# RWKV mixer: low-rank products in two passes over high and low parts, and unit norms of k made in the projections

## The chip, the cores and the metric

The kernel runs on one core of a Trainium2 chip. A time is the device time of one execution in microseconds (us). The kernel before has a median of 3618.76 us over 3 runs (3618.49 to 3623.94).

## The reference, cut to what matters

The model has two blocks. The first holds a mixer of attention and mLSTM, an MLP, an RWKV mixer and a second MLP; the second block has gated linear attention and a mixture of experts. Only the RWKV mixer is touched here. It works on 768 tokens (512 latent, 256 context) of width 1024, that is 16 heads of 64.

```python
def rwkv_prepare(h, mu, w_rkv, w0, w1, w2, a0, a1, a2, g1, g2, k_k, k_a):
    xx = centred_shift(h) - h
    xr, xw, xk, xv, xa, xg = h[None] + xx[None] * mu[:, None, None, :]
    r, k, v = jnp.einsum('sbtd,sde->sbte', jnp.stack([xr, xk, xv]), w_rkv)
    w_logit = w0[:, None, None, :] + jnp.einsum('zbtr,zrd->zbtd', jnp.tanh(jnp.einsum('btd,zdr->zbtr', xw, w1)), w2)
    decay = jnp.exp(-jnp.exp(-jax.nn.softplus(-w_logit.astype(jnp.float32)) - 0.5))
    a = jax.nn.sigmoid(a0[:, None, None, :] + jnp.einsum('zbtr,zrd->zbtd', jnp.einsum('btd,zdr->zbtr', xa, a1), a2))
    g = jax.nn.sigmoid(xg @ g1) @ g2
    kk = split_heads((k * k_k).astype(jnp.float32), RW_HEADS, RW_HEAD_DIM)
    kk = (kk / jnp.maximum(jnp.linalg.norm(kk, axis=-1, keepdims=True), 1e-12)).reshape(k.shape)
    k_dir = k[None] * (1.0 + (a - 1.0) * k_a)
    return r, k_dir, v, decay, -kk, kk[None] * a, g
```

The index z is the direction of the recurrence (forward, backward), the rank r is 64. Each head then runs a recurrence over the tokens in both directions with a 64 x 64 state: `s = s * w + (s a) b' + v k'`, and reads it with r.

## The kernel before, in words

Tensors lie transposed: 128 channels (one feature block f, two heads) on the partitions and 768 tokens along the free axis. `PARTS` cuts the tokens into 512 and 256, one PSUM bank each.

*Projections* (`rw_mixer`). `stream(i, parts)` makes the shifted input of one projection (L1159, VectorE) and splits it into a high part xh (ScalarE, rounded to fp32r) and the rest xl (VectorE). `split` and `load_w` do the same with weights, the low part on GpSimd (L479). `dense` multiplies high by high, high by low and low by high in fp32r passes (L500). `project` yields the PSUM tile of each block; the order of the streams is k, v, w1, a1, r, g1. `keep` copies a block out and stores it. For k, `sqk` is the square of k times `k_k`, and a product with the constant `kks` (L1189) sums the squares of each head into two held banks. After the last block a square root (L1193), a maximum (L1194) and a reciprocal (L1195) leave the inverse norms of all 16 heads in `kkn`. `tw` and `ta` are the 2 x 64 inner values of the two low-rank pairs, in fp32, direction z on partitions 64z to 64z + 63.

*Recurrences* (`rw_scan`). A block is loaded by `head(f)`: k, v, r, and 128 x 128 blocks `w2` and `a2`. The product with the constant `kkb` (L1318) spreads the block's two inverse norms over its 128 channels, and VectorE multiplies (L1319) to get `nkk`. `rw_pre(j)` handles one direction z of one block (j = 2f + z). In it `lora2` makes one fp32 product of contraction 64 for each part (L1446), and ScalarE evicts it with a tanh (L1447). Then come a running sum along the tokens (`cs`), exponentials (L1456, L1457), the scaled operands (L1484 to L1497), Gram products (L1532), an inverse by halves (L1600 to L1635), the outputs (L1681 to L1769), and the chain of states S (L1354, L1362). `rw_pre` of j + 3 is written beside the work on j, so that the pieces of several j overlap; each engine takes its instructions in one fixed order, settled when the program is built.

*PSUM in the recurrences*: banks of tag b rotate by two among L1318, L1446, the Gram products and the chain. The 19 memsets of L1271 clear the block-diagonal tiles on GpSimd before the first block. `keep = {KD-2: tw, KD-1: ta}` in `rw_scan` reuses `tw` and `ta` for the outputs of the last two blocks.

Of the kernel before, what the change touches and what calls it, by code (L numbers as in the profile page):

```python
# [10 lines left out]
F32 = mybir.dt.float32  # L11
F32R = mybir.dt.float32r
# [7 lines left out]
T = 512  # L20
# [97 lines left out]
def constants_rw():  # L118
# [12 lines left out]
    ks = np.zeros((128, 2, 32)); kb = np.zeros((128, 2, 128))  # L131
    for i in range(2):
        for h in range(2):
            ks[64 * h:64 * h + 64, i, 2 * i + h] = 1.0
            kb[2 * i + h::32, i, 64 * h:64 * h + 64] = 1.0
    b.add("kks", ks)
    b.add("kkb", kb)
# [108 lines left out]
def layout(v):  # L246
# [21 lines left out]
    for n in ("w2", "a2"):  # L268
        o["rw_" + n] = np.ascontiguousarray(v["rw_" + n][0].reshape(128, D))
# [43 lines left out]
class Kern:  # L313
# [336 lines left out]
    def ab_mixer(self):  # L650
# [24 lines left out]
        with ExitStack() as st:  # L675
            cp = st.enter_context(tc.tile_pool(name="ab_c", bufs=1, reuse_waits="tile"))
            pool = st.enter_context(tc.tile_pool(name="ab", bufs=2, reuse_waits="tile"))
# [343 lines left out]
    def ml_head(self, h, qkv, ntile, tmp, out):  # L1021
# [34 lines left out]
        for n in range(6):  # L1056
            for d in range(2):
# [11 lines left out]
                if n < 5:  # L1069
                    ns = self.small.tile([128, 130], F32, tag="cst", name=self.uid("cst"), bufs=4)  # L1070
# [6 lines left out]
                if n:  # L1077
                    t = self.small.tile([128, 130], F32, tag="hin", name=self.uid("hin"), bufs=2)
                    nc.scalar.activation(t, pn[:, 130:260], AF.Copy, scale=col("wi", c, d))
                    nc.vector.tensor_tensor(num[d][:, c, :], pn[:, :130], t, op=ALU.add)  # L1080
# [31 lines left out]
    def rw_mixer(self):  # L1112
# [3 lines left out]
        with ExitStack() as st:  # L1116
# [8 lines left out]
            spill = {n: [dr.tile([128, TT], F32, name=f"d_{n}{f}") for f in range(8)] for n in ("x", "r", "k", "v", "g", "o")}  # L1125
            tw = cp.tile([128, TT], F32, name="tw")
            ta = cp.tile([128, TT], F32, name="ta")
            kkn = cp.tile([128, TT], F32, name="kkn")
            with tc.tile_pool(name="rw1", bufs=2, reuse_waits="tile") as pool:
# [45 lines left out]
                def keep(n, f, ps, lo, hi):  # L1175
                    t = pool.tile([128, TT], F32, tag="tmp", name=self.uid("keep"), bufs=self.tb)
                    nc.scalar.activation(t[:, lo:hi], ps[:, lo:hi], AF.Copy)
                    nc.sync.dma_start(spill[n][f][:, lo:hi], t[:, lo:hi])

                act = stream(2, PARTS)  # L1180
                self.x = None
                ssk = [self.bank("ssk"), self.bank("ssk")]
                for f, ps in project(act, self.i["rw_k"], KD, PARTS):
                    keep("k", f, ps, 0, TT)
                    sq = pool.tile([128, TT], F32, tag="tmp", name=self.uid("sqk"), bufs=self.tb)
                    nc.scalar.activation(sq, ps, AF.Square, scale=self.p("k_k")[:, f:f + 1])
                    g = f % 4
                    for q, (a, b) in enumerate(PARTS):
# [3 lines left out]
                for q, (a, b) in enumerate(PARTS):  # L1192
# [1213 lines left out]
```

## Time and profile before

| | |
|---|---|
| median of 3 runs | 3618.76 us |
| profiled execution | 3612.26 us |
| its span | 3610.2 us |
| TensorE clock, mean over the span | 0.956 of full |
| projections of RWKV | 1172 to 1476 us |
| recurrences of RWKV | 1476 to 2249 us |
| output projection, MLP, second block | from 2249 us |
| DMA traffic in the 36th to 39th of 40 slices | 421 GB/s |

The profiled execution is 2.06 us longer than its span. Busy time counts instructions that work on data; an engine's idle time is what it waits. A busy TensorE does not mean a TensorE at full speed: the granted clock is read beside it.

### The profile page before, as it was taken

To read this page: it belongs to the slowest core of one execution; us is meant where nothing else is said; L and a number is where in the kernel's file an instruction comes from. 1 tells how busy PE (TensorE), PEld (TensorE's weight loads), DVE (VectorE), ACT (ScalarE), POOL (GpSimd) and SP (SyncE) were. 2 spreads that over 40 slices of the span, in tenths; PEclk is the share of its full clock that TensorE was granted. 3 is DMA by queue.
4 is the path that set the end of the run, shared out by engine and by line. 5 is a ranking of instruction groups with operands and counts; after the bars stand their busy time and mean duration, and the time that the engine had idled before them with its cause. 6 is when DMAs were issued, how large, how long until landed. Compare 5 with 4: busy or idle time off the path is not lost. (4 is left out here: it accounts for less than half of the span.)

```text
span 3610.2 us, 56697 instructions
## 1 busy us (share of the span) xinstructions
PE 3285.7 (91%) x23614; PEld 2459.9 (68%) x23614; DVE 1748.3 (48%) x3056; ACT 1303.4 (36%) x2465; POOL 898.1 (25%) x460
## 2 busy tenths in 40 slices
PE   7999999999999898799999998889999989799887
PEld 5767887888888676477777776677878767433333
DVE  5475564861322324576666674474333564222213
ACT  3332453221222324376667765322233453100001
POOL 1111113232223422422222220444452334200000
PEclk9999999999999899699999998999999999899999
DMA  5212222552213122100000002475331226699998
GB/s 215 99 65 82 82 71 94 198 170 65 65 60 116 62 90 75 56 15 21 21 21 21 21 8 68 135 231 177 95 127 64 69 87 230 254 421 421 421 421 317
DMA packets 125071, 480.86 MB, mean 133 GB/s; under 512 B 13232, under 2 KB 24944, under 8 KB 100496
## 3 DMA queue, kind: packets, MB, share of 16 engines
q1 hardware_dynamic: 118688, 469.68, 35.9%
q8 instruction: 186, 3.05, 0.3%
q0 software_dynamic: 1184, 4.20, 0.3%
q10 hardware_dynamic: 4944, 3.36, 0.3%
q14 instruction: 69, 0.57, 0.0%
HBM read 451.50 MB, written 25.69 MB: 132 GB/s over the span
## 5 line engine op out<-in xcount | busy, mean ns | idle before, releaser
L479 POOL TENSOR_TENSOR wl<-w,wh 128x1024 fp32r<-128x1024 f32 (+1 forms) x258 | 617.4, 2395 | 1633.9 <-ACT wh L478 1477.8
L478 ACT ACTIVATE wh<-w 128x1024 fp32r<-128x1024 f32 (+1 forms) x258 | 265.8, 1032 | 950.1 <-PE dn L500 332.0
L500 PE MATMUL dn<-hh,wh 128*128 128x512 f32 (+1 forms) x768 | 234.1, 359 | 14.2 <-ACT hh L478 14.2
L500 PE MATMUL up<-ah,wh 128*128 128x512 f32 (+1 forms) x768 | 235.1, 361 | 7.2 <-DVE x L591 3.0
L500 PE MATMUL up<-ah,wl 128*128 128x512 f32 (+1 forms) x768 | 236.0, 362 | 4.8 <-POOL wl L479 4.5
L500 PE MATMUL dn<-hl,wh 128*128 128x512 f32 (+1 forms) x768 | 235.7, 361 | 2.2 <-DVE hl L479 2.2
L500 PE MATMUL dn<-hh,wl 128*128 128x512 f32 (+1 forms) x768 | 234.9, 360 | 2.4 <-POOL wl L479 2.4
L500 PE MATMUL up<-al,wh 128*128 128x512 f32 (+1 forms) x768 | 236.2, 362 | 0.6 <-DVE al L584 0.6
L467 DVE SCALAR_TENSOR_TENSOR side<-wside,condb 128x1024 f32<-128x1024 f32 x128 | 193.2, 1509 | 65.6 <-DMA wside<-ada 64.3
L623 DVE TENSOR_TENSOR u<-u 128x768 f32<-128x768 f32 (+1 forms) x64 | 126.6, 1980 | 131.9 <-ACT u L622 131.9
L591 DVE SCALAR_TENSOR_TENSOR x<-dn,ada,x 128x512 f32<-128x512 f32 x96 | 60.5, 657 | 257.4 <-PE dn L500 257.4
L500 PEld LDWEIGHTS dn<-hh,wh 128*128 128x128 f32 x768 | 128.0, 190 | 39.3 <-ACT hh L478 15.8
L500 PEld LDWEIGHTS up<-ah,wh 128*128 128x128 f32 x768 | 129.0, 191 | 32.8 <-ACT ah L583 3.9
L500 PEld LDWEIGHTS up<-ah,wl 128*128 128x128 f32 x768 | 128.5, 190 | 30.9 <-POOL wl L479 8.5
L500 PEld LDWEIGHTS dn<-hl,wh 128*128 128x128 f32 x768 | 128.7, 190 | 25.6 <-DVE hl L479 4.1
L500 PEld LDWEIGHTS dn<-hh,wl 128*128 128x128 f32 x768 | 128.4, 190 | 26.0 <-POOL wl L479 3.3
L500 PEld LDWEIGHTS up<-al,wh 128*128 128x128 f32 x768 | 129.5, 191 | 23.7 <-DVE al L584 1.8
L500 PE MATMUL rp<-xh,wh 128*128 128x512 f32 (+1 forms) x368 | 112.0, 371 | 23.0 <-ACT xh L478 20.6
L500 PE MATMUL rp<-xl,wh 128*128 128x512 f32 x368 | 113.2, 373 | 13.9 <-DVE xl L479 13.8
L478 ACT ACTIVATE hh<-u 128x768 fp32r<-128x768 f32 (+1 forms) x64 | 47.3, 739 | 217.2 <-DVE u L623 217.2
L500 PE MATMUL p<-ah,wh 128*128 128x512 f32 (+1 forms) x320 | 116.9, 394 | 2.2 <-ACT ah L583 1.2
L500 PE MATMUL rp<-xh,wl 128*128 128x512 f32 x368 | 112.4, 370 | 3.0 <-POOL wl L479 3.0
(612 smaller groups left out, 7471.6 us busy)
## 6 DMA issues: line engine op xcount, KB each, us to landing
w<-mlp SPq DMA_DIRECT2D x128, 512.0 KB, 3.6
wside<-ada SPq DMA_DIRECT2D x96, 512.0 KB, 3.8
ew<-e_gate SPq DMA_DIRECT2D x45, 1024.0 KB, 19.8
ew<-e_up SPq DMA_DIRECT2D x41, 1024.0 KB, 20.6
ew<-e_down SPq DMA_DIRECT2D x39, 1024.0 KB, 19.8
wada<-ada SPq DMA_DIRECT2D x48, 512.0 KB, 3.8
ewm<-e_up SPq DMA_DIRECT2D x18, 1024.0 KB, 19.8
ewm<-e_down SPq DMA_DIRECT2D x18, 1024.0 KB, 19.8
```

Source lines behind the costliest of these rows:

```text
L467: nc.vector.scalar_tensor_tensor(o, w, 1.0, cb[:, q, :], op0=ALU.mult, op1=ALU.mult, accum_out=out[:, f, q:q + 1])
L478: nc.scalar.activation(hi, src, AF.Copy)
L479: (eng or nc.vector).tensor_tensor(lo, src, hi.bitcast(F32), op=ALU.subtract)
L500: nc.tensor.matmul(ps[:, a:b], ww[:, 128 * k:128 * k + 128], aa[:, a:b], start=(first and k == 0 and q == 0), stop=(last and k == nk - 1 a ...
L591: self.nc.vector.scalar_tensor_tensor(x[:, a:b], ps[:, a:b], gt[:, f, q:q + 1], x[:, a:b], op0=ALU.mult, op1=ALU.add)
L623: nc.vector.tensor_tensor(u[:, lo:hi], u[:, lo:hi], u[:, lo:hi], op=ALU.mult)
```

## The change

The second factors of both low-rank pairs come as one array `rw_l2`: for each block 128 x 512, four blocks of 128 columns (two tables, two directions), with the 64 rows repeated on the other 64 partitions. `head` loads it into the tile of tag y and splits it: high part l2h on ScalarE, low part l2l on GpSimd. The inner values become two tiles each, one for a direction: `factors` writes the high part on partitions 64z and following, and the rest on the other 64. A product over all 128 partitions with l2h and one with l2l then sum all four combinations of the parts. The inverse norm is made per block in the projections by `unit`, called one block late, and -k k_k / norm goes to memory and is loaded as `nkk`. Two new tiles `ends` take the place of `tw` and `ta` for the last outputs. The tiles cst and hin of the first mixer move from one pool to another.

```diff
-    for n in ("w2", "a2"):
-        o["rw_" + n] = np.ascontiguousarray(v["rw_" + n][0].reshape(128, D))
+    l2 = np.stack([v["rw_w2"][0], v["rw_a2"][0]])
+    l2 = np.concatenate([l2, l2], 2).reshape(2, 2, 128, KD, 128).transpose(3, 2, 0, 1, 4)
+    o["rw_l2"] = np.ascontiguousarray(l2.reshape(KD, 128, 512))
...
+                def factors(out, ps, func):
+                    t = pool.tile([128, TT], F32, tag="tmp", name=self.uid("fac"), bufs=self.tb)
+                    nc.scalar.activation(t, ps, func)
+                    for z, h in enumerate(out):
+                        r, o = slice(64 * z, 64 * z + 64), slice(64 - 64 * z, 128 - 64 * z)
+                        nc.scalar.activation(h[r], t[r], AF.Copy)
+                        nc.vector.tensor_tensor(h[o], t[r], h[r].bitcast(F32), op=ALU.subtract)
...
-                ssk = [self.bank("ssk"), self.bank("ssk")]
+                def unit(f, t, sq):
+                    for a, b in PARTS:
+                        pk = self.bank("ssk")
+                        nc.tensor.matmul(pk[:, :b - a], C["hones"], sq[:, a:b], start=True, stop=True)
+                        nc.scalar.activation(sq[:, a:b], pk[:, :b - a], AF.Sqrt)
+                    nc.vector.tensor_scalar(sq, sq, 1e-12, -1.0, op0=ALU.max, op1=ALU.mult)
+                    nc.vector.reciprocal(sq, sq)
+                    nc.vector.scalar_tensor_tensor(sq, t, self.p("k_k")[:, f:f + 1], sq, op0=ALU.mult, op1=ALU.mult)
+                    nc.sync.dma_start(spill["kk"][f], sq)
+                late = None
                 for f, ps in project(act, self.i["rw_k"], KD, PARTS):
-                    keep("k", f, ps, 0, TT)
+                    t = keep("k", f, ps, 0, TT)
                     sq = pool.tile([128, TT], F32, tag="tmp", name=self.uid("sqk"), bufs=self.tb)
                     nc.scalar.activation(sq, ps, AF.Square, scale=self.p("k_k")[:, f:f + 1])
...
-                        nc.tensor.matmul(ssk[q][32 * g:32 * g + 32, :b - a],
-                                         C["kks"].rearrange("p (i m) -> p i m", i=2)[:, f // 4, :], sq[:, a:b],
-                                         start=(f < 4), stop=(f >= 4), skip_group_check=True)
+                    if late:
+                        late()
+                    late = partial(unit, f, t, sq)
...
-                    nc.scalar.activation(kkn[:, a:b], ssk[q][:, :b - a], AF.Sqrt)
-                nc.vector.tensor_scalar(kkn, kkn, 1e-12, -1.0, op0=ALU.max, op1=ALU.mult)
-                nc.vector.reciprocal(kkn, kkn)
...
                 for f, ps in project(act, self.i["rw_v"], KD, PARTS):
                     keep("v", f, ps, 0, TT)
+                    if late:
+                        late = late()
...
-                    nc.scalar.activation(tw, ps, AF.Tanh)
+                    factors(tw, ps, AF.Tanh)
...
-                    nc.scalar.activation(ta, ps, AF.Copy)
+                    factors(ta, ps, AF.Copy)
...
         def head(f):
-            w2 = pool.tile([128, 128], F32, tag="w2", name=self.uid("w2"), bufs=1)
-            a2 = pool.tile([128, 128], F32, tag="a2", name=self.uid("a2"), bufs=1)
-            nc.sync.dma_start(w2, self.i["rw_w2"][:, fc])
-            nc.sync.dma_start(a2, self.i["rw_a2"][:, fc])
             nkk = role("nkk")
-            for a, b in PARTS:
-                pk = self.pbank("b")
-                nc.tensor.matmul(pk[:, :b - a], kb[gi:gi + 32, f // 4, :], kkn[gi:gi + 32, a:b], start=True, stop=True)
-                nc.vector.scalar_tensor_tensor(nkk[:, a:b], k[:, a:b], self.p("k_k")[:, f:f + 1], pk[:, :b - a],
-                                               op0=ALU.mult, op1=ALU.mult)
+            nc.sync.dma_start(nkk, spill["kk"][f])
+            raw = role("y", T)
+            nc.sync.dma_start(raw, self.i["rw_l2"][f])
+            wh = pool.tile([128, 4, 128], F32R, tag="l2h", name=self.uid("l2h"), bufs=1)
+            wl = pool.tile([128, 4, 128], F32R, tag="l2l", name=self.uid("l2l"), bufs=1)
+            self.split(raw, wh.rearrange("p n m -> p (n m)"), wl.rearrange("p n m -> p (n m)"), nc.gpsimd)
...
         def lora2(n, t, bias, name):
             o = e1(name)
             for a, b in PARTS:
                 ps = self.pbank("b")
-                nc.tensor.matmul(ps[:, :b - a], w[zr, :], t[zr, a:b], start=True, stop=True)
+                for q, w in enumerate(hd["l2"]):
+                    nc.tensor.matmul(ps[:, :b - a], w[:, 2 * n + z, :], t[z][:, a:b], start=(q == 0), stop=(q == 1))
                 nc.scalar.activation(o[:, a:b], ps[:, :b - a], AF.Tanh, scale=0.5, bias=bias)
```

The order on TensorE at the low-rank products of direction 0 of block 2 (the period from 1615 us), before. The first names are PSUM banks; consts and crw hold constants, ar, kd, bh and ad belong to the outputs of an earlier j:

```order
L1318 MATMUL b_12927<-kkn,crw 128x512
L1715 MATMUL d_13061<-vx_11218,ak_11212 64x64 x4
L1681 MATMUL d_13074<-ar_11741,kd_11208 128x128
L1318 MATMUL b_12930<-kkn,crw 128x256
L1681 MATMUL d_13074<-ar_11741,kd_11208 128x128
L1446 MATMUL b_12934<-tw,w_2026_12922 128x512
L1446 MATMUL b_12937<-tw,w_2026_12922 128x256
L1681 MATMUL d_13074<-ar_11741,kd_11208 128x128 x2
L1446 MATMUL b_12941<-ta,a_2027_12923 128x512
L1446 MATMUL b_12944<-ta,a_2027_12923 128x256
L1746 MATMUL d_13084<-bh_13039,ad_11214 128x128 x4
```

And now (L1452 is the low-rank product, L1687 was L1681, L1752 was L1746, L1710 was L1704):

```order
L1687 MATMUL d_13164<-ar_11825,kd_11287 128x128 x2
L1452 MATMUL b_13020<-tw_9327,l2h_13015 128x512
L1452 MATMUL b_13020<-tw_9327,l2l_13016 128x512
L1687 MATMUL d_13164<-ar_11825,kd_11287 128x128 x2
L1452 MATMUL b_13024<-tw_9327,l2h_13015 128x256
L1452 MATMUL b_13024<-tw_9327,l2l_13016 128x256
L1752 MATMUL d_13174<-bh_13129,ad_11293 128x128
L1452 MATMUL b_13029<-ta_9329,l2h_13015 128x512
L1452 MATMUL b_13029<-ta_9329,l2l_13016 128x512
L1452 MATMUL b_13033<-ta_9329,l2h_13015 128x256
L1452 MATMUL b_13033<-ta_9329,l2l_13016 128x256
L1752 MATMUL d_13174<-bh_13129,ad_11293 128x128 x3
```

The two products with kkn are gone, each low-rank part is a pair of passes, and one more group of other products stands between the parts.

The order on GpSimd at the start of the recurrences, the last of the memsets and what follows, before:

```order
L1271 MEMSET zb_11236 128x1536
L1271 MEMSET zb_11238 128x1536
L1271 MEMSET lo 128x1536
L1494 TENSOR_SCALAR al_11286<-al_11286,half 128x768
L1495 TENSOR_TENSOR al_11286<-al_11286,k_11263 128x768
L1497 TENSOR_TENSOR kd_11206<-al_11286,wl_11279 64x12x64
```

And now:

```order
L1284 MEMSET zb_11315 128x1536
L1284 MEMSET zb_11317 128x1536
L1284 MEMSET lo 128x1536
L474 TENSOR_TENSOR l2l_11352<-y_11349,l2h_11351 128x512
L1500 TENSOR_SCALAR al_11364<-al_11364,half 128x768
L1501 TENSOR_TENSOR al_11364<-al_11364,k_11342 128x768
L1503 TENSOR_TENSOR kd_11285<-al_11364,wl_11355 64x12x64
```

The low part of block 0's weights (l2l) stands behind the memsets and ahead of the first al.

The order on VectorE at the turn from the stream of k to that of v (xs and xl are v's inputs and their low parts), before:

```order
L1159 SCALAR_TENSOR_TENSOR xs_9999<-xx_9363,params,x_4577 128x768
L1194 TENSOR_SCALAR kkn<-kkn 128x768
L479 TENSOR_TENSOR xl_9989<-xs_9987,xh_9988 128x768
L1195 RECIPROCAL kkn<-kkn 128x768
L479 TENSOR_TENSOR xl_9995<-xs_9993,xh_9994 128x768
L479 TENSOR_TENSOR xl_10001<-xs_9999,xh_10000 128x768
```

And now, where sqk_9964 is the unit of block 6:

```order
L1155 SCALAR_TENSOR_TENSOR xs_10052<-xx_9363,params,x_4576 128x768
L1194 TENSOR_SCALAR sqk_9964<-sqk_9964 128x768
L474 TENSOR_TENSOR xl_10048<-xs_10046,xh_10047 128x768
L1195 RECIPROCAL sqk_9964<-sqk_9964 128x768
L474 TENSOR_TENSOR xl_10054<-xs_10052,xh_10053 128x768
L1196 SCALAR_TENSOR_TENSOR sqk_9964<-keep_9961,params,sqk_9964 128x768
L1155 SCALAR_TENSOR_TENSOR xs_10058<-xx_9374,params,x_4577 128x768
```

The reciprocal stands at the same place between v's first two low parts, with another block's data; a multiplication follows the second low part. The reciprocal of block 7 has moved behind the last of v's low parts.

## Rows read from the trace of the kernel before

**Rows 1.** The page, part 1: busy time, share of the span and instructions.

```profile
PE 3285.7 (91%) x23614; PEld 2459.9 (68%) x23614; DVE 1748.3 (48%) x3056; ACT 1303.4 (36%) x2465; POOL 898.1 (25%) x460
```

**Rows 2.** Busy time in stretches of the projections and recurrences: (x) are instructions, then clock.

```profile
1183.00:1476.00 293.00, 257.70 (x1163) 195.10 (x1163) 104.25 (x122) 97.63 (x128) 88.50 (x64) 0.94 0.22 76
1476.50:1541.00 64.50, 40.62 (x369) 28.70 (x367) 39.49 (x53) 25.03 (x58) 32.81 (x23) 0.63 0.15 47
1541.00:1615.10 74.10, 66.29 (x1039) 53.80 (x1038) 53.88 (x87) 53.16 (x141) 23.50 (x11) 0.95 0.05 13
1615.10:1704.30 89.20, 84.44 (x1296) 67.75 (x1296) 62.29 (x122) 63.49 (x160) 20.96 (x10) 0.98 0.07 21
1704.30:1796.30 92.00, 87.68 (x1295) 69.62 (x1295) 62.23 (x121) 63.41 (x160) 20.95 (x10) 0.94 0.07 21
1799.90:1811.00 11.10, 11.10 (x63) 7.51 (x62) 4.83 (x9) 4.65 (x8) 0.00 (x0) 0.54 0.00 0
```

**Rows 3.** Timeline of TensorE, blocks from 1615 and 1796: start, duration, line, form.

```profile
1615.15 1.12 PE L1318 MATMUL b<-kkn,crw 32*128 32x512 f32 x2 [0.24 <-DVE vx L1333]
...
1617.00 0.69 PE L1318 MATMUL b<-kkn,crw 32*128 32x256 f32 x2
...
1618.04 1.55 PE L1446 MATMUL b<-tw,w 64*128 64x512 f32 x4
1619.53 0.71 PE L1681 MATMUL d<-ar,kd 128*128 128x128 f32 x4
...
1802.61 2.93 PE L1446 MATMUL b<-ta,a 64*128 64x512 f32 x4
```

**Rows 4.** Timeline of TensorE in the dense stream of v.

```profile
1299.69 0.52 PE L500 MATMUL rp<-xh,wh 128*128 128x512 f32 x2
1300.05 0.52 PE L500 MATMUL rp<-xl,wh 128*128 128x512 f32 x2
```

**Rows 5.** Timeline of ScalarE at the evictions of the same products.

```profile
1619.26 1.05 ACT L1447 ACTIVATE wl<-b,half 128x512 f32<-128x512 f32 x2 [1.80 <-PE b L1446]
```

**Rows 6.** Timeline of GpSimd at the start of the recurrences.

```profile
1489.87 1.38 POOL L1271 MEMSET lo<- 128x1536 f16 x1
```

**Rows 7.** Groups of GpSimd, shapes apart: count, busy, mean ns, idle before.

```profile
L479 POOL TENSOR_TENSOR wl<-w,wh 128x512 fp32r<-128x512 f32 x16 | 21.2, 1329 | 30.8 <-ACT wh L478 30.4 <-DMA w<-gla_proj 0.5
```

**Rows 8.** Timelines of TensorE and ScalarE at the start of the recurrences.

```profile
1483.05 2.90 PE L1446 MATMUL b<-tw,w 64*128 64x512 f32 x4 [4.76 <-DVE ar L1485]
...
1498.14 2.26 PE L1532 MATMUL b<-ar,bd 128*128 128x128 f32 x9 [4.71 <-DVE bd L1492]
...
1490.62 0.84 ACT L1456 ACTIVATE wl<-cs 128x768 f32<-128x768 f32 x1
```

**Rows 9.** Timelines of VectorE and TensorE at the turn from k to v.

```profile
1281.71 0.96 DVE L479 TENSOR_TENSOR xl<-xs,xh 128x768 fp32r<-128x768 f32 x1 [0.17 <-ACT xh L478]
1282.58 4.95 DVE L1195 RECIPROCAL kkn<-kkn 128x768 f32<-128x768 f32 x1
...
1288.39 1.01 PE L500 MATMUL rp<-xl,wh 128*128 128x512 f32 x2 [3.29 <-DVE xl L479]
```

**Rows 10.** Timelines of VectorE and TensorE at the turn from w1 to a1.

```profile
1373.26 6.81 DVE L1159 SCALAR_TENSOR_TENSOR xs<-xx,params,x 128x768 f32<-128x768 f32 x5
...
1377.70 0.62 PE L500 MATMUL rp<-xh,wh 128*128 128x512 f32 x2 [2.88 <-ACT xh L478]
1380.99 1.01 PE L500 MATMUL rp<-xl,wh 128*128 128x512 f32 x2 [2.68 <-DVE xl L479]
```

**Rows 11.** Timeline of the loads and stores that SyncE issues.

```profile
1749.13 0.32 SPq L1390 DMA_DIRECT2D d_o<-y  x1
...
1758.19 0.33 SPq L1310 DMA_DIRECT2D w<-rw_w  x1
```

**Rows 12.** Line 1492 by itself: count, duration min/median/max, first and last start.

```profile
L1492 DVE SCALAR_TENSOR_TENSOR bd<-nkk,cs x32: 949/1242/2489, 1496.1 to 2141.7; 64x768 f32<-64x768 f32 x32
```

**Rows 13.** The page, part 5: a group of weight loads in a dense stream.

```profile
L500 PEld LDWEIGHTS dn<-hh,wh 128*128 128x128 f32 x768 | 128.0, 190 | 39.3 <-ACT hh L478 15.8
```

More of the change, by code (lines that the diff above doesn't have):

```diff
@@ L130, in constants_rw @@
     b.add("hones", hb)
[L131 to L137, printed above, removed]
     return b
@@ L676, in ab_mixer @@
             cp = st.enter_context(tc.tile_pool(name="ab_c", bufs=1, reuse_waits="tile"))
-            pool = st.enter_context(tc.tile_pool(name="ab", bufs=2, reuse_waits="tile"))
+            pool = self.abp = st.enter_context(tc.tile_pool(name="ab", bufs=2, reuse_waits="tile"))
             nab = self.i["c_ab"].shape[1]
@@ L1069, in ml_head @@
                 if n < 5:
-                    ns = self.small.tile([128, 130], F32, tag="cst", name=self.uid("cst"), bufs=4)
+                    ns = self.abp.tile([128, 130], F32, tag="cst", name=self.uid("cst"), bufs=4)
                     if n == 0:
@@ L1077, in ml_head @@
                 if n:
-                    t = self.small.tile([128, 130], F32, tag="hin", name=self.uid("hin"), bufs=2)
+                    t = self.abp.tile([128, 130], F32, tag="hin", name=self.uid("hin"), bufs=2)
                     nc.scalar.activation(t, pn[:, 130:260], AF.Copy, scale=col("wi", c, d))
@@ L1124, in rw_mixer @@
             H = {n: crh[:, a:b] for n, (a, b) in self.crwh.items()}
[L1125 to L1128, printed above, removed]
+            spill = {n: [dr.tile([128, TT], F32, name=f"d_{n}{f}") for f in range(8)] for n in ("x", "r", "k", "kk", "v", "g", "o")}
+            tw = [cp.tile([128, TT], F32R, name=f"tw{z}") for z in range(2)]
+            ta = [cp.tile([128, TT], F32R, name=f"ta{z}") for z in range(2)]
+            ends = [cp.tile([128, T], F32, name=f"end{i}") for i in range(2)]
             with tc.tile_pool(name="rw1", bufs=2, reuse_waits="tile") as pool:
@@ L1224, in rw_mixer @@
                 self.ps = s2.enter_context(tc.tile_pool(name="ps2", bufs=1, space=PSUM, reuse_waits="tile"))
-                self.rw_scan(pool, C, H, spill, (tw, ta, kkn))
+                self.rw_scan(pool, C, H, spill, (tw, ta, ends))
             self.open_w()
@@ L1237, in rw_mixer @@
                     else:
-                        t = (tw, ta)[k - KD + 2][:, :T]
+                        t = ends[k - KD + 2]
                     h = pool.tile([128, T], F32R, tag="oh", name=self.uid("oh"), bufs=KD)
@@ L1263, in rw_scan @@
         nc = self.nc
-        tw, ta, kkn = small
-        keep = {KD - 2: tw, KD - 1: ta}
+        tw, ta, ends = small
+        keep = {KD - 2: ends[0], KD - 1: ends[1]}
         def diag(n, c=12, dt=F32):
@@ L1445, in lora2 @@
                 ps = self.pbank("b")
[L1446 removed]
+                for q, w in enumerate(hd["l2"]):
+                    nc.tensor.matmul(ps[:, :b - a], w[:, 2 * n + z, :], t[z][:, a:b], start=(q == 0), stop=(q == 1))
                 nc.scalar.activation(o[:, a:b], ps[:, :b - a], AF.Tanh, scale=0.5, bias=bias)
             return o
[L1450 to L1451 removed]
+        sg = lora2(0, per["tw"], half[:, z, f:f + 1], "wl")
+        th = lora2(1, per["ta"], half[:, 2 + z, f:f + 1], "al")
         nc.vector.tensor_scalar(sg, sg, 1.0, None, op0=ALU.add)
```

14 lines of the change are left out of this document (3 added, 11 removed).

## The prediction

> **What bounds the kernel now.** I read the page's busy shares first: TensorE is busy 91% of the span, VectorE 48%, ScalarE 36%, GpSimd 25% [rows 1]. An average is no proof, so I read the stage that the change touches by the busy time of each engine in stretches: the projections of the RWKV mixer, and then the recurrences, one stretch for each feature block f (a pair of heads; its period runs from one broadcast of the k norms to the next) [rows 2]. In blocks 2 to 7 TensorE works 84.4 of 89.2 us or 87.7 of 92.0 us, VectorE 62 and ScalarE 63. The pipeline is not full in block 0 (40.6 of 64.5 us) and nearly full in block 1 (66.3 of 74.1). The end of the program waits for expert weights; their loads follow the stages before them, so I let an earlier end of RWKV come through whole.
>
> The reader is to see a second thing in rows 2: periods of 92.0 us have mean clock 0.94, those of 89.2 us 0.98. The difference is a spell at half clock. The stretch 1799.9 to 1811 has a granted clock of 0.54 and TensorE busy for all of 11.1 us [rows 2]; the low-rank product that takes 1.55 us elsewhere takes 2.93 there [rows 3]. So the engine is at 1.2 GHz instead of 2.4 for about 10 us. The spell begins in the broadcast and the low-rank products of direction 0, in four of blocks 2 to 7 (those from 1704, 1796, 1888 and 2069; the two from 1615 and 1980 have none). It also gives an exchange rate: such a block has 87.68 − 84.44 = 3.24 us more TensorE time and a period 2.8 us longer (92.0 − 89.2), so a microsecond of TensorE is worth some 0.87 of period.
>
> **The change, part by part.** *Broadcast of the k norms (L1318).* For each block two products go, of 512 and 256 columns: 1.12 and 0.69 us [rows 3]. Modelled ends reach past the next start by some 0.06 (the low-rank product from 1618.04 lasts 1.55 and the next begins at 1619.53), so 1.69 us go. The two VectorE multiplications behind them go too; VectorE is not the bound.
>
> *Low-rank products (L1446).* There are four per block, two tables for two directions. One of 512 + 256 columns takes 1619.53 − 1618.04 = 1.49 us to the next start [rows 3]. The nearest fp32r row is the dense stream, where one pass over 512 + 256 columns takes 1300.05 − 1299.69 = 0.36 us [rows 4]; two passes take 0.72 in a stream. A product that stands alone also pays for a change of operands: I add 0.2 us as an estimate (two bare parts, 1.12 + 0.69, cost 0.26 more than the joined 1.55), so 0.92, or 0.57 saved. Four save 2.28 us; one more break in the row order of direction 0 (the order shown with the change) takes 0.2 back. Together with the broadcast: 3.77 us of TensorE per block. Bounds: nothing saved on the low-rank part (1.69 in all) and the pure stream figures (4 × 0.77 + 1.69 = 4.77).
>
> *Eviction.* ScalarE's two tanh of a product take 1.05 us [rows 5], longer than the new 0.92 of TensorE, and two banks rotate. A third part can then wait some 0.3 us for its bank. I count this in the factor 0.87 and not apart.
>
> So blocks 2 to 7 give 6 × 3.77 × 0.87 = 19.7 us. In block 1 the pipeline fills and I take a third, 1.3; block 0 nothing, since TensorE waits there 24 of 64 us. Sum −21.0.
>
> *The spells.* They cost 4 × 2.8 = 11.2 us. The stretch in which they begin loses over a third of its TensorE time, and what is left there runs over all 128 rows of the array rather than 32 or 64. A start that occurs in four blocks of six is near an edge. I take them as gone, −11.2; the other ends are 0 and a loss (third rival).
>
> *Start of the recurrences.* GpSimd's first work there is 19 memsets (L1271); the last ends at 1489.87 + 1.38 = 1491.25 [rows 6]. The low part of block 0's weights is now made on GpSimd, behind all of them in its queue. A split of that size took 1.33 us [rows 7], so it is ready at about 1492.6. Before, the first low-rank product began at 1483.05 and the exponential behind it at 1490.62 [rows 8]. After it: the high passes can go early; the four low passes (0.3), the tanh evictions (two of 1.05 us, about 2.4 with their semaphores) and the table load (1.3, the gap ahead of 1490.62) lead to an exponential at 1496 to 1496.5. So +5.5 us, which the Gram product at 1498.14 [rows 8] follows. Ends: 0, if the memsets start earlier, and 1492.6 − 1483.05 = 9.5.
>
> *Norms made in the projections.* The new unit of a block has an fp32 product of the same columns as the sums that it replaces, two square roots, a scalar operation and a multiplication (about 1.6 with the 0.96 of a 128 × 768 operation), a reciprocal of 4.95 us [rows 9] and a store. Eight units are 52 us of VectorE, in a stage where it works 104 of 293 us [rows 2], and its wait for the k stream covers those of blocks 0 to 5. The unit is delayed by one block, so its product no longer waits for the square. At the turn from k to v the old chain holds TensorE until 1288.39, because the low half of v's second input sits behind the reciprocal from 1282.58 [rows 9]. The new order keeps one reciprocal, block 6's, at that place (order shown), and block 7's comes when v's inputs are made. I take 0, ends −5 and +4. If that cover went, each reciprocal on the path would cost 4.95.
>
> *Splitting tanh(x w1) and x a1.* Each gets two ScalarE copies and two VectorE subtractions over 64 partitions. The nearest row is a VectorE run of five preparing operations, 6.81 us, at 1373.26, after which TensorE waits 2.88 us (for ScalarE) and 2.68 us (for VectorE) [rows 10]: here VectorE does bound. Two subtractions are about 1.9 us by that 0.96. The second turn (a1 to r) is alike. I take +1.5 each, +3; ends 0 and 7.
>
> *Loads of a block.* Two small weight loads become one of 256 KB into the tile of the readout, whose last reader is the store at 1749.13; the old loads went out from 1758.19 on [rows 11] and their use is at 1799. The k norms come as one load more. Landing, and the splits on ScalarE and on GpSimd (1.33 us), have some 40 us; nothing. GpSimd's split can hold VectorE up: L1492 takes 0.95 us at best and 2.49 at worst [rows 12], and GpSimd works 21 us in each block. With 27 us of VectorE free per block I leave that out; were all of it on the path, the sum would lose 8 × 1.33 = 10.6 us.
> The Trainium skill, SBUF — State Buffer, section "Who interferes with whom", says that a VectorE instruction with two inputs in SBUF and a GpSimd one that reads SBUF exclude each other; the spread of L1492 agrees, and at its worst the rule gives those 10.6 us.
>
> **Sum:** −21.0 − 11.2 + 5.5 + 3.0 = −23.7 us on the profiled execution's 3612.26 (its span of 3610.2 and 2.06 around it), giving 3588.6. The median of the runs is 3618.76, 6.5 higher (0.18%); the gain belongs to either, so the forecast is 3595.1. Less than 0.2% (7.2 us) is what a measurement can't tell from no change.
>
> **Rivals.** *First: the spells stay or move.* For it: what is left of the low-rank work is still dense, and nothing else in the block changes. Then −12.5, 3606.3.
>
> *Second: the period is held by the chain of waits, not by TensorE.* VectorE and ScalarE work 62 and 63 of 89 us, much of it one after the other through TensorE; if only a third of the 21.0 us comes through, and the spells' time turns into waiting, the sum is −7 + 8.5 = +1.5, 3620. Against it: the rate of 0.87.
>
> *Third, the slower side: more spells.* The clock falls after every set of low-rank products, 16 of them (two directions, eight blocks), instead of 4, since waits for banks and evictions now stand in them. At 2.8 us each, 12 more cost 33.6 us and the sum is −12.5 + 33.6 = +21, 3640. It decides from eleven spells on (7 more are +19.6 against −12.5, so +7.1). For it: the engine is near the edge. Against: the products of direction 1 have none today.
>
> *Fourth: weight loads exposed.* The dense stream changes weights at each pass, all of 128 rows, and still makes a pass in 0.36 us [rows 4], though a load takes 190 ns [rows 13]. Were each of a product's four loads exposed, it would take 0.92 + 0.76 = 1.68, more than 1.49; a block would save 0.9 instead of 3.77, and with spells as they are the sum is −4.8 + 8.5 = +4, 3622.
> The Trainium skill, TensorE: Matmul & The Clock Gate, section "The mechanism", says that a weight load overlaps running products only where the row group differs, which speaks against this change: its passes use all rows, the old ones half. By that rule 3622; the row has full-height loads hidden, and it decides.
>
> **How the numbers follow.** Forecast 0.46 (own range 3585 to 3603), spells stay 0.26 (3600 to 3613), chain-bound 0.15 (3611 to 3628), more spells 0.09, loads exposed 0.04. The range 3580 to 3615 leaves out the last two and part of the third. Faster: 0.46 + 0.25 + 0.05 of the third = 0.76; same: 0.01 + 0.09 + 0.04 = 0.14; slower: 0.09 + 0.01 = 0.10.
>
> **What would show it.** Right: no L1318; periods of 85 to 86.5 us in blocks 2 to 7, all alike; a low-rank product of 0.9 us; a first exponential near 1496 us, give or take what the projections shift; the last expert loads earlier by the whole gain. Wrong: periods that keep two values some 2.8 us apart (first rival), a period near 89 with TensorE's idle time grown (second), half-clock stretches in every block and direction (third), or 1.7 us per product (fourth).

## The result, and the profile after

The changed kernel has a median of 3583.97 us over 4 runs (3578.87 to 3585.53); the kernel before had 3620.43 (3618.49 to 3623.94) over 4. The ratio is 0.9898, with an interval of 0.9886 to 0.991: some 36 us faster. The two profiled executions stand 28.4 us apart (3612.26 and 3583.87). The profiled execution of before is faster than all of its four timed runs; that of after lies at the median of its own.

First the page's line of busy times, which answers [rows 1]:

```profile
PE 3238.9 (90%) x23582; PEld 2448.4 (68%) x23582; DVE 1791.7 (50%) x3066; ACT 1312.9 (37%) x2491; POOL 908.3 (25%) x468
```

TensorE lost 46.8 us of work, VectorE gained 43. Now the stretches that answer [rows 2], in the same columns; a block's period begins here with its load of v, which before started within half a microsecond of the broadcast from block 2 on:

```profile
1483.40:1543.60 60.20, 27.24 (x246) 20.76 (x246) 30.41 (x43) 20.06 (x44) 33.14 (x23) 0.56 0.21 64
1543.60:1627.30 83.70, 73.41 (x1168) 61.91 (x1166) 61.40 (x93) 60.33 (x161) 25.62 (x13) 0.93 0.06 19
1627.30:1715.40 88.10, 80.75 (x1277) 67.20 (x1277) 65.17 (x120) 62.60 (x158) 21.91 (x11) 0.96 0.09 27
1800.75:1885.74 84.99, 79.22 (x1291) 66.92 (x1291) 60.80 (x120) 63.30 (x161) 22.60 (x11) 0.98 0.10 29
1885.74:1970.74 85.00, 79.21 (x1291) 66.80 (x1291) 60.82 (x120) 63.29 (x161) 22.61 (x11) 0.98 0.10 28
1869.50:1872.90 3.40, 3.40 (x25) 2.67 (x26) 1.90 (x5) 2.11 (x7) 0.00 (x0) 0.50 0.31 87
```

The steady block takes 85.0 us with 79.2 of TensorE, in place of 89.2 with 84.4 or 92.0 with 87.7. The spell of 10 us is gone in all of blocks 2 to 7, but the last row shows that short ones are left: 3.4 us at a granted clock of 0.50, 1.2 GHz, one in each block and two in blocks 2 and 3. Block 1, where before had only two short ones, now holds a long one:

```profile
1562.30:1572.50 10.20, 9.12 (x103) 8.08 (x103) 7.70 (x9) 5.91 (x18) 6.09 (x3) 0.50 0.01 2
```

All periods, from the starts of the loads of v:

| block | 0 | 1 | 2 | 3 | 4 | 5 | 6 |
|---|---|---|---|---|---|---|---|
| before | 53.6 | 83.1 | 89.2 | 92.0 | 92.0 | 92.0 | 89.2 |
| after | 59.7 | 83.7 | 88.1 | 85.4 | 85.0 | 85.0 | 85.0 |

The low-rank products of direction 0 on TensorE, which answer [rows 3]:

```profile
1885.95 0.50 PE L1452 MATMUL b<-tw,l2h 128*128 128x512 f32 x1 [0.24 <-DVE vx L1340]
1886.29 0.40 PE L1452 MATMUL b<-tw,l2l 128*128 128x512 f32 x1
1886.62 0.45 PE L1721 MATMUL d<-vx,ak 128*64 128x64 f32 x8
1887.00 0.71 PE L1687 MATMUL d<-ar,kd 128*128 128x128 f32 x4
1887.69 0.38 PE L1452 MATMUL b<-tw,l2h 128*128 128x256 f32 x1
1887.91 0.28 PE L1452 MATMUL b<-tw,l2l 128*128 128x256 f32 x1
1888.02 0.43 PE L1452 MATMUL b<-ta,l2h 128*128 128x512 f32 x1
```

A pass of 512 columns takes some 0.33 us to the next start here and one of 256 0.11 to 0.22. By themselves, the 16 fp32 low-rank instructions of a block before and the 16 passes now (busy time of TensorE and of its weight loads, then clock):

```profile
1615.10:1704.30 89.20, 6.48 (x16) 2.60 (x16) 0.98 0.07 21
1885.74:1970.74 85.00, 4.22 (x16) 2.59 (x16) 0.98 0.10 28
```

So the passes hold TensorE for 4.2 us; before, the fp32 instructions and the broadcast held it for 6.5 + 1.8 = 8.3.

The start of the recurrences on GpSimd, ScalarE and TensorE, in this order, which answers [rows 6, 8]:

```profile
1493.91 1.37 POOL L1284 MEMSET lo<- 128x1536 f16 x1
1495.25 1.26 POOL L474 TENSOR_TENSOR l2l<-y,l2h 128x512 fp32r<-128x512 f32 x1
...
1491.47 0.63 ACT L473 ACTIVATE l2h<-y 128x512 fp32r<-128x512 f32 x1 [8.48 <-DMA y<-rw_l]
...
1502.20 0.84 ACT L1462 ACTIVATE wl<-cs 128x768 f32<-128x768 f32 x1
...
1492.16 1.00 PE L1452 MATMUL b<-tw,l2h 128*128 128x512 f32 x2 [9.53 <-ACT l2h L473]
1496.56 1.01 PE L1452 MATMUL b<-tw,l2l 128*128 128x512 f32 x2 [3.40 <-POOL l2l L474]
...
1509.72 2.68 PE L1538 MATMUL b<-ar,bd 128*128 128x128 f32 x11 [4.71 <-DVE bd L1498]
```

The high passes went at 1492.16, as soon as ScalarE had split the weights, and the low ones waited 3.40 us for GpSimd, whose split stood behind the memsets. The weights themselves came late: their load is the fifth of the block's six.

### The profile page after: what moved, and what is told of

It reads as the page before. It is cut to its first block, busy times and chain, and to the rows that moved or that the text cites. A ratio compares the mean times of both kernels' runs of the same rounds, so it can differ in the third digit from the quotient of the medians.

```text
span 3581.7 us, 56701 instructions
## 1 busy us (share of the span) xinstructions
PE 3238.9 (90%) x23582; PEld 2448.4 (68%) x23582; DVE 1791.7 (50%) x3066; ACT 1312.9 (37%) x2491; POOL 908.3 (25%) x468
## 5 line engine op out<-in xcount | busy, mean ns | idle before, releaser
L495 PE MATMUL rp<-xh,wh 128*128 128x512 f32 x368 | 111.1, 373 | 23.3 <-ACT xh L473 21.5
L495 PE MATMUL p<-ah,wl 128*128 128x512 f32 x320 | 113.3, 383 | 2.1 <-POOL wl L474 2.1
```

The costliest lines, as they stand in the source:

```text
L495: nc.tensor.matmul(ps[:, a:b], ww[:, 128 * k:128 * k + 128], aa[:, a:b], start=(first and k == 0 and q == 0), stop=(last and k == nk - 1 a ...
```

## The experiments

Profiled executions differ outside the change too: that of after reached the mixer's first instructions 6.3 us late, and gained 6.1 us in the last stage, where the experts' weights came at 426 GB/s instead of 421. So stages are compared below by their own lengths. From the mixer's first instructions to the loads of its output projection after is 28.3 us shorter than before; the other two differences nearly cancel.

**Each half alone.** The low-rank change alone keeps kkn and the broadcast:

```diff
-                nc.tensor.matmul(ps[:, :b - a], w[zr, :], t[zr, a:b], start=True, stop=True)
+                for q, w in enumerate(hd["l2"]):
+                    nc.tensor.matmul(ps[:, :b - a], w[:, 2 * n + z, :], t[z][:, a:b], start=(q == 0), stop=(q == 1))
```

> Only the low-rank products in two passes; the norms of k stay as before (held sums, one reciprocal, two broadcast products per block). Because of memory the output of block 6 goes through DRAM. Theory (the period of a block is TensorE's time, one to one, and the half-clock spell begins in the run of fp32 products over 32 and 64 rows): blocks 2 to 7 without a spell take 85.0 + 1.7 = 86.7 us; with the low-rank products no longer fp32 the run is too short and no 10 us spell is left. Program some 15 us faster than before, 13 slower than the full change. Rival A (the broadcast over 32 rows starts the spells): some blocks at 89 to 90 us, program only 5 to 8 us faster than before. Rival B (a chain of waits sets the period): periods near 85 again, program within 4 us of the full change.

The norms change alone keeps the fp32 products and has `unit` and the load of `nkk`:

```diff
-                nc.tensor.matmul(pk[:, :b - a], kb[gi:gi + 32, f // 4, :], kkn[gi:gi + 32, a:b], start=True, stop=True)
...
+            nc.sync.dma_start(nkk, spill["kk"][f])
```

> Only the norms of k made in the projections; the low-rank products stay fp32 over 64 rows with two small weight loads. Theory: blocks 2 to 7 take 85.0 + 2.4 = 87.4 us without a spell; the first exponential comes some 6 us sooner after the scan's loads than in the full change, and the two splits in the projections are gone (about 3 us); program some 18 us faster than before if the spells go, 8 if they stay. Rival A (the broadcast starts the spells): no spells left, all blocks alike. If the low-rank products alone start them: two kinds of blocks, 87.4 and 90.2. Rival B (chain of waits): periods of 85, program faster than the full change by 9 us.

The low-rank change alone: 3622.57 us, ratio 1.0016 (1.0004 to 1.0027), no gain at all. The norms alone: 3589.76, ratio 0.9916 (0.9902 to 0.9929). A block of each; the first holds one 3.4 us spell (clock 0.98), the second none (1.00):

```profile
1992.78:2081.64 88.86, 81.44 (x1296) 67.62 (x1296) 65.80 (x122) 63.39 (x160) 21.81 (x11) 0.98 0.08 23
```

```profile
1799.88:1886.18 86.30, 81.16 (x1291) 65.83 (x1291) 61.20 (x120) 63.30 (x160) 20.95 (x10) 1.00 0.09 27
```

With the low-rank change alone TensorE worked 81.4 us per block, 3.0 less than before, but the period stayed at 88.9 to 90.9: idle time rose from 4.8 to 7.4 us. So the theory fell for this half. Spells of 6.8 or 10.2 us also stayed in three of its blocks 2 to 6. The norms alone left no spell above 3.4 us in blocks 2 to 6 and added little wait (5.1 us of idle time for 4.8). Their blocks with one short spell (2, 3 and 6) take 87.8 us against 89.2 before, 1.4 us for 1.8 us of broadcast; the blocks at 86.3 have lost the short spell as well. The two gains don't add: the norms alone bring 29 of the 36 us, the low-rank products nothing by themselves and some 6 beside the norms. That long spells stay with the broadcast and go without it is what the rival of the broadcast asked for. Where the low-rank change lost time is in the waits of TensorE, in VectorE's timeline and in GpSimd's (columns of the waits: sum, times, longest):

```profile
PE b L1348 <- DVE vx L1351: 2.1, 1, 2.1
```

```profile
1988.28 2.47 DVE L1559 TENSOR_TENSOR zb<-hi,crwh 64x768 f16<-64x768 f16 x2 [1.24 <-POOL hi L1557]
1990.67 0.95 DVE L1561 TENSOR_TENSOR lo<-Aab,hi 64x768 f16<-64x768 f32 x1
1991.65 0.74 DVE L1351 COPY vx<-b 64x256 f32<-64x256 f32 x2
...
1985.66 2.58 POOL L1557 TENSOR_TENSOR hi<-Aab,crw 64x768 f16<-64x768 f32 x1 [11.79 <-PE b L1566]
1988.32 2.01 POOL L1561 TENSOR_TENSOR lo<-Aab,hi 64x768 f16<-64x768 f32 x1
```

VectorE's two zb operations took 2.47 us together, with GpSimd's lo beside them from 1988.32 on; the copy of v's transposes (vx, 1991.65) came that much later, and TensorE stood 2.1 us. Before, two zb take 1.14 us, and lo waited for TensorE and began only after them:

```profile
1699.59 1.14 DVE L1542 TENSOR_TENSOR zb<-hi,crwh 64x768 f16<-64x768 f16 x2 [1.72 <-POOL hi L1540]
...
1700.97 2.35 POOL L1544 TENSOR_TENSOR lo<-Aab,hi 64x768 f16<-64x768 f32 x1 [1.42 <-PE i L1629]
```

**That meeting taken away.** Both halves of lo on VectorE, on the low-rank change alone:

```diff
-            (nc.gpsimd, nc.vector)[h].tensor_tensor(lo[row(h), :, h, :], Aab[row(h)], hi[row(h), :, h, :], op=ALU.subtract)
+            nc.vector.tensor_tensor(lo[row(h), :, h, :], Aab[row(h)], hi[row(h), :, h, :], op=ALU.subtract)
```

> The low-rank change alone once more, with both halves of `lo` (the low part in the inverse) made on VectorE, so that GpSimd no longer reads memory beside VectorE's zb there. In the low-rank change alone TensorE's busy time fell by 3 us per block against before and its idle time rose by 2.7; zb took 0.89 us on average instead of 0.55, and the transposes of v behind it waited 2.1 us. Theory (the two engines exclude each other there, and that wait ate the gain): zb back at 0.55 us, the wait at L1348 below 0.5 us, undisturbed blocks at 87.3 to 88 us instead of 88.9, program some 8 us faster than the low-rank change alone. Rival (the order of the instructions as a whole makes the waits): zb may shorten, but idle time stays near 7.4 us per block and the period within 0.5 us.

3596.27 us, ratio 0.9939 (0.9922 to 0.9956): 26 us less than the low-rank change alone, three times what was expected. zb, the groups of both kernels over four blocks (count, busy, mean ns), and a block:

```profile
L1559 DVE TENSOR_TENSOR zb<-hi,crwh 64x768 f16<-64x768 f16 x16 | 14.2, 890 | 5.2 <-POOL hi L1557 5.0
```

```profile
L1559 DVE TENSOR_TENSOR zb<-hi,crwh 64x768 f16<-64x768 f16 x16 | 8.9, 553 | 7.2 <-POOL hi L1557 6.8
```

```profile
1718.57:1804.95 86.38, 80.52 (x1296) 67.28 (x1296) 63.82 (x124) 63.42 (x161) 17.83 (x9) 0.98 0.08 23
```

zb is back at 0.55 us, idle time at 5.9 and the period at 86.4. TensorE's busy time fell too, and in blocks 2 to 6 no spell is longer than 3.4 us any more, where the low-rank change alone had three; so the size is not the meeting's alone, and its share is not separated. Two controls make the same edit elsewhere.

> The kernel before, with both halves of `lo` on VectorE: the control of the run in which that move made the low-rank change alone 26 us faster. Theory (the move helped there because GpSimd's lo met VectorE's zb): before has no such meeting (zb 0.55 us), so blocks stay at 89 to 92 us and the program within 5 us of before. Rival (GpSimd's lo costs every version, through its own slowness): blocks 2 to 7 shorter by 1 us and more each, program 6 us or more faster than before.

3619.26 us, ratio 1.0 (0.9988 to 1.0012): where zb and lo don't meet, the edit brings nothing. The traced execution is the slowest of the ten (3637.69), with blocks of 90.2 to 94.9 us, above the 89 to 92 expected.

> The kernel with the early split (block 0's weights first, split on VectorE) with both halves of `lo` on VectorE. Theory (no meeting there): within 3 us of the early split alone. Rival (GpSimd's lo costs every version): 6 us or more faster.

3577.77 us (3574.85 to 3579.74), against 3573.42 (3570.86 to 3577.89) of the same kernel without it (below): 4.4 us slower by the medians, where within 3 were expected, and not the rival's 6 us faster. A small meeting did go there, zb from 0.62 to 0.55 us on average, and brought nothing.

**TensorE's time doubled back.** One low pass more in each low-rank part:

```diff
-                for q, w in enumerate(hd["l2"]):
+                for q, w in enumerate(hd["l2"] + hd["l2"][1:]):
```

> The full change with the low pass done twice (the low part of the weights counts double): four products more passes of 0.36 us, 1.44 us of TensorE per block and nothing else. Theory (rate one to one): periods of 86.4 us in place of 85.0, program 10 to 11 us slower than the full change. By the rate that the prediction took (0.87): 86.25, 9 to 10 us. Rival B (a chain of waits sets the period): 85.0 to 85.3, program within 2 us.

3591.24 us, 7.3 above the change by the medians; the RWKV part of the profiled execution is 9.4 us longer. A block without any spell:

```profile
1889.19:1975.25 86.06, 79.75 (x1299) 66.90 (x1299) 63.46 (x120) 63.93 (x161) 22.28 (x11) 1.00 0.09 28
```

So time added to these products comes through to the end, and the rival that a chain of waits sets the period whatever TensorE does is out. It is no clean one to one: with the early split (below) a block at a clock of 1.00 takes 82.9 us with 77.4 of TensorE, so 2.3 us more of TensorE came with 3.2 us of period, and VectorE's bd grew from 1.60 to 1.98 us on average. A chain that runs through these very products would lengthen too; the run does not part it from TensorE's load.

**The start.** Block 0's weights are loaded first and split on VectorE:

```diff
+            raw = role("y", T)
+            if f == 0:
+                nc.sync.dma_start(raw, self.i["rw_l2"][f])
             r, k, v = role("r", T), role("k"), role("v")
...
-            self.split(raw, wh.rearrange("p n m -> p (n m)"), wl.rearrange("p n m -> p (n m)"), nc.gpsimd)
+            self.split(raw, wh.rearrange("p n m -> p (n m)"), wl.rearrange("p n m -> p (n m)"), nc.gpsimd if f else None)
```

> The full change, but block 0's weights are loaded ahead of its other loads and their low part is made on VectorE, not on GpSimd behind the memsets. Theory (the memsets hold the first low-rank product): its low pass starts at about 1493 instead of 1496.6 or earlier by the load, everything behind it 4 to 5 us sooner, program 4 to 5 us faster than the full change. Rival (something else ends last at the start: the loads of k norms, or GpSimd's queue): the first Gram product moves by less than 1 us and the program by nothing that can be told.

3573.42 us (3570.86 to 3577.89), ratio 0.9872 (0.9857 to 0.9887): the fastest kernel here, 10.5 us under the change and 45.6 under before. VectorE, TensorE and ScalarE at the start:

```profile
1487.88 0.69 DVE L474 TENSOR_TENSOR l2l<-y,l2h 128x512 fp32r<-128x512 f32 x1 [20.61 <-ACT l2h L473]
...
1487.90 1.01 PE L1454 MATMUL b<-tw,l2h 128*128 128x512 f32 x2 [4.36 <-ACT l2h L473]
1488.70 0.93 PE L1454 MATMUL b<-tw,l2l 128*128 128x512 f32 x2
...
1502.29 0.98 PE L1540 MATMUL b<-ar,bd 128*128 128x128 f32 x3 [6.93 <-DVE bd L1500]
...
1495.11 0.84 ACT L1464 ACTIVATE wl<-cs 128x768 f32<-128x768 f32 x1
```

The low passes follow the high ones at once, and block 0 takes 48.6 us in place of 59.7, twice the expected gain: beside the memsets the late load of the weights had cost time. Counted from the load of v, the low passes come 9.3 us sooner and the high ones 5.7; the run changes load and split together and does not part their shares. Blocks 4 to 6 are as in the change, block 2 takes 86.9 us for 88.1, and block 3 shows what a block without any spell takes:

```profile
1704.55:1787.42 82.87, 77.41 (x1293) 65.62 (x1292) 60.24 (x119) 62.62 (x158) 22.58 (x11) 1.00 0.10 29
1787.42:1872.39 84.97, 79.23 (x1291) 66.82 (x1291) 60.77 (x120) 63.28 (x161) 22.59 (x11) 0.98 0.10 29
```

82.9 us at a clock of 1.00 against 85.0 at 0.98: one 3.4 us spell goes with 2.1 us of period here, and with 1.4 to 1.6 in the norms alone (87.7 to 87.9 against 86.3).

**The splits in the projections.** The four subtractions of `factors` moved to GpSimd, on the kernel with the early split:

```diff
-                        nc.vector.tensor_tensor(h[o], t[r], h[r].bitcast(F32), op=ALU.subtract)
+                        nc.gpsimd.tensor_tensor(h[o], t[r], h[r].bitcast(F32), op=ALU.subtract)
```

> The kernel with block 0's weights first and split on VectorE, and in the projections the four subtractions of the inner values moved from VectorE to GpSimd. Theory (VectorE bounds the turns w1 to a1 to r, and the splits cost some 4 us there): the first store of r comes 2 to 4 us sooner after the last of v, program 2 to 4 us faster than with the early split alone. Rival (the subtractions fall into waits anyway, or GpSimd's slower ones hold VectorE through the shared memory side): within 1 us or slower.

3578.72 us, 5.3 slower than without. From the last store of v to the first of r it takes 56.3 us, against 51.4 with the subtractions on VectorE, 51.7 in the change, and 47.2 before. GpSimd needs 4.32 us for two subtractions, VectorE 1.94, and beside it single operations of VectorE that take 1.0 us elsewhere take 2.56 and 2.57. The rival held.

**What starts the long spell.** Two pairs, equal in the order of TensorE's instructions but for two pairs of neighbours in the second, add a product of zeros with 512 + 256 columns to the low-rank product of tw in direction 0, over 32 rows and over 128. First on the full change:

```diff
+                    if q == 0 and n == 0 and z == 0:
+                        nc.tensor.matmul(ps[:64, :b - a], per["z32"][:32], t[z].bitcast(F32)[:32, a:b], start=False, stop=False)
```

> The full change with one fp32 product more per part in the low-rank product of tw in direction 0: 32 rows, 64 columns of weights that are all zero, 512 + 256 columns streamed; the sums stay what they are. It brings back the shape of the broadcast of the k norms (1.7 us of TensorE per block), without its eviction. Theory (products over few rows start the spell): periods 85 + 1.7 = 86.7 us where no long spell is, and spells of 7 to 10 us in several blocks, program 15 to 25 us slower than the full change. Rival (only TensorE's time counts): all blocks 86.7, program 13 us slower, same as with 128 rows.

> As the 32-row kernel, with the same order on every engine, but the zero product runs over all 128 rows. Theory (few rows start the spell): no spell of 7 us or more in blocks 2 to 7, periods 86.7 us, program 12 to 14 us slower than the full change and 5 to 10 faster than the 32-row kernel. Rival (rows do not matter): same periods and clock as with 32 rows, within 1 us per block.

3600.76 us with 32 rows and 3597.82 with 128 (ratios 0.9952 and 0.9951): no difference. A block of each, 32 rows first:

```profile
1719.77:1805.51 85.74, 80.17 (x1295) 66.50 (x1295) 61.12 (x120) 63.53 (x161) 22.38 (x11) 1.00 0.10 28
1713.70:1799.44 85.74, 80.17 (x1295) 66.49 (x1295) 61.12 (x120) 63.53 (x161) 22.38 (x11) 1.00 0.10 28
```

Neither has a spell over 3.4 us in blocks 2 to 6. Rows did not matter there, the rival's side. Then on the norms alone, where the fp32 products of tw and ta stand around the added one, so that the run is as long as before:

> The norms change alone, with a zero product over 32 rows (512 + 256 columns, 64 columns of weights) behind each part of the first fp32 low-rank product of direction 0. So the run of fp32 products over few rows is as long as before, only the broadcast's eviction is missing. Theory now (a long run of fp32 products, however few or many rows, starts the long spell; two of its three parts are not enough): spells of 7 to 10 us come back in several blocks, periods 88 without and 90 to 91 with one, program 15 us slower than the norms alone. Rival (zero data or a missing eviction keeps the clock up; the long spell belongs to the old order): no spell over 4 us, periods 88 to 89.5.

> As the run before, with the zero product over 128 rows. If rows don't matter, as in the pair on the full change: the same periods and spells within 1 us per block. If rows matter where the run is long: long spells with 32 rows and none with 128, 2 to 3 us per block between them.

3613.74 us with 32 rows (ratio 0.9985, 0.9975 to 0.9995) and 3600.91 with 128 (0.9951, 0.994 to 0.9963). Two blocks of each, and the spell and the products in it with 32 rows:

```profile
1617.42:1707.20 89.78, 85.34 (x1295) 68.53 (x1295) 61.31 (x120) 63.20 (x160) 20.93 (x10) 0.96 0.09 25
1707.20:1798.66 91.46, 87.03 (x1295) 69.27 (x1295) 61.40 (x120) 63.32 (x160) 20.94 (x10) 0.94 0.09 25
1711.30:1718.10 6.80, 6.80 (x34) 5.37 (x32) 4.56 (x8) 3.49 (x6) 0.00 (x0) 0.50 0.01 2
```

```profile
1621.62:1710.43 88.81, 83.91 (x1295) 67.02 (x1295) 61.31 (x120) 63.41 (x160) 20.97 (x10) 0.98 0.09 26
1710.43:1799.24 88.81, 83.90 (x1295) 67.00 (x1295) 61.41 (x120) 63.42 (x160) 20.97 (x10) 0.98 0.09 26
```

```profile
1707.41 1.12 PE L1453 MATMUL b<-tw,w 64*128 64x512 f32 x2 [0.24 <-DVE vx L1339]
1708.46 1.07 PE L1455 MATMUL b<-tw,zero 32*64 32x512 f32 x2
1709.46 0.70 PE L1453 MATMUL b<-tw,w 64*128 64x256 f32 x2
1710.09 0.64 PE L1455 MATMUL b<-tw,zero 32*64 32x256 f32 x2
1710.66 2.29 PE L1453 MATMUL b<-ta,a 64*128 64x512 f32 x4
```

With 32 rows a half-clock stretch begins in the low-rank product of ta (2.29 us from 1710.66, for 1.55 at full speed) or just behind it and lasts 3.4 or 6.8 us, in each of blocks 2 to 7; with 128 rows it is not there. So the theory of the first of these two runs, that rows don't matter in a long run, fell, and in this order they do. What TensorE did before the clock fell was this: fp32 products over 32 and 64 rows, one after the other. It is one traced execution of each; the medians, 12.8 us apart, fit. In the low-rank change alone a spell begins in the broadcast itself, but TensorE had stood for 2 us just before:

```profile
1721.26 0.63 PE L1348 MATMUL b<-consts,v 128*64 128x128 f32 x4 [2.14 <-DVE vx L1351]
1721.82 1.90 PE L1330 MATMUL b<-kkn,crw 32*128 32x512 f32 x2
```

The 1.90 us are 1.12 at full speed. Few rows are not the only start: the short spell at a block's end is there with 128 rows too (once 6.8 us long), and block 1 of the full change holds 10.2 us without any broadcast. Why a spell lasts 10 us in one version and 3.4 in another stays open.

## Why the prediction was right, and where it was not

The direction, the place and the order of the terms held: the gain lies in blocks 2 to 7, the start and the turns give some back. The time lies 11 us under the forecast, inside its range of 3580 to 3615 and 1 us below the narrower one of the forecast itself (3585 to 3603). Term by term, from the profiled executions:

| term | forecast | measured |
|---|---|---|
| blocks 2 to 7, products and spells | −30.9 | −34.3 |
| block 1 | −1.3 | +0.6 |
| block 0, start | +5.5 | +6.2 |
| projections, norms and splits | +3.0 | −0.7 |
| sum (before rounding) | −23.7 | −28.3 |

*Blocks 2 to 7.* 25.9 us of it are the difference of the periods of blocks 2 to 6 (454.4 against 428.5), 8.4 block 7 up to the loads of the output projection. A block with one short spell took 89.2 us before and takes 85.0 now, 4.2 us where the sum had 3.77 × 0.87 = 3.3. The saving in the changed products was sized well (8.3 − 4.2 = 4.1 us per block), and by them alone the exchange is one to one. But TensorE's whole busy time, from which the rate of 0.87 had been read, fell by 84.4 − 79.2 = 5.2 us: by that measure the rate is 0.81 and held, and what the sum lacks is 1.1 us of busy time in other products. Which reading is right no run shows. In the sum the low-rank products give more than the norms' broadcast; the runs of the halves show that most of the time came with the norms, through the broadcast and the long spells together.

*The long spells* went in blocks 2 to 7, as forecast. The reason given, fewer columns and no few-row products, holds as far as the pairs go: with both put back (norms alone, 32 rows) they return in part, with one of them (full change, 32 rows) they don't. What I did not count are the short spells. Each block keeps one of 3.4 us, at its end and not in the low-rank products, worth 1.4 to 2.1 us; the blocks of 89.2 us, with a clock of 0.98, had one too, though the prediction calls them free of spells. Block 2, with two of them, took 88.1 us, outside the 85 to 86.5 that I asked of all blocks.

*Block 1* was to gain 1.3 us and lost 0.6. It now holds the spell of 10.2 us shown above; what starts it no run shows.

*Start.* The mechanism and the size were right (5.5 and 6.2; the first exponential comes 6.0 us later after the load of v): the low passes waited for GpSimd behind the memsets. The late load beside it, for which the high passes waited, I had left out; the early split takes away both.

*Projections.* The splits cost 4.5 us up to the first store of r (51.7 against 47.2 us from the last store of v), where I had 3. Up to the first load of block 0 it is 119.95 us before, 120.94 after and 117.62 with the norms alone, so by that pair 3.3 remain. The norms were to be free and gave 1.7 us, counted from the mixer's first instructions to the last store of v. TensorE's waits for a square were to vanish and fell from 3.6 to 2.3 us, which accounts for part of it. Of the units' 52 us on VectorE nothing shows; the cover held.

*Rivals.* The chain of waits is real, though it did not decide in this kernel (idle time per block went from 4.8 to 5.8 us): when the low-rank products were changed alone, waits and the spells that stayed ate their whole gain. The rule of exclusion on the shared memory side that I had left out of the sum had a part there: zb and lo met, and two zb took 1.3 us longer while TensorE stood 2.1 us. The Trainium skill, SBUF — State Buffer, section "Who interferes with whom", says just this of two-input VectorE instructions beside GpSimd's reads, and the pair of 0.89 and 0.55 us agrees. Exposed weight loads did not come: passes with changed weights follow each other by 0.33 us, and a product takes 4.2 / 4 = 1.05 us, near the 0.92 of the sum and not 1.68; so the rule on row groups that the prediction cites (the Trainium skill, TensorE: Matmul & The Clock Gate, section "The mechanism") would have been wrong here. That rival's own sum left out the extra break: with it a block would save 0.7 us, not 0.9.

*The base.* 4.6 of the 11 us between forecast and result are in the table; the other 6.5 are the base. I set the gain on the median of the runs, and the profile of before was a quick execution (3612.26; 46 later runs gave 3612.04 to 3625.76, with medians of 3616.75 to 3619.54), that of after a median one. The longer executions of before have the lower mean clock (0.957 in the two shortest of its last 24 runs, 0.954 and 0.955 in the two longest), so they may hold more spells than the traced one; with no trace of them that stays open. How far a kernel scatters does not follow from the spells in its trace: the norms alone lie within 3589.27 and 3591.99, but the norms with 128 rows of zeros, without the spells of the low-rank products, within 3595.61 and 3613.01.

## What to carry to other kernels

Before you read from two blocks what a saved microsecond is worth, see that they hold the same clock spells: the norms seem worth 2.9 us when a block without a spell is set against one with a spell, and 1.4 when both have one. Look also which engine's instruction starts beside which after the edit: half of this change was worth nothing alone, in part because it let a GpSimd read meet a VectorE one. A helper operation put on an idle engine stands behind everything that engine still has in its queue, so look at the first use as well as the steady one. Forecast against several executions of the kernel before, since one profile can lie 7 us off their median.

## What the runs showed of the hardware

- fp32 products over 32 and 64 rows in a run were followed by a granted clock of 0.50 for 3.4 or 6.8 us in each of blocks 2 to 7; with 128 in place of 32 rows they were not (periods 89.7 and 91.5 us against 88.8 to 90.1; one traced execution of each).
- An fp32 product takes the same time over 32 and over 128 rows (0.61 and 0.62 us per instruction of 512 columns, 0.40 and 0.40 of 256, in the pair on the full change).
- Two fp32r passes over 128 rows cost 0.65 of one fp32 product over 64 rows (4.2 against 6.5 us per block).
- Two zb operations of VectorE took 2.47 us beside a GpSimd subtraction that reads the same memory, 1.14 without.
- GpSimd took 4.32 us for two subtractions of 64 x 768 beside VectorE's work, VectorE 1.94.
